# Four whole chunks beside nine pairs in the down stages of a two-layer encoder kernel

## The chip, the cores and the metric

The kernel is one program on one core of a Trainium2 chip. The metric is the device time of one execution in microseconds. The engines of the core work in parallel, each in the order of its own instruction queue: TensorE (PE: matmuls; PEld: its weight loads), VectorE (DVE), ScalarE (ACT), GpSimd (POOL) and SyncE (SP, which here issues DMAs). They wait for each other through semaphores. POOL issues DMAs too, among them those that add what they bring to what lies in SBUF (accumulating DMAs).

## The reference

An encoder of two layers on 512 positions of width 1024, all in float32. Each layer has two feed-forward parts, an attention part between them and an embedding gate at the end. The change touches the feed-forward parts alone, and of them the end of the up projection and the whole down projection:

```python
def swiglu(x, w_gate, w_up, w_down):
    return (jax.nn.silu(x @ w_gate) * (x @ w_up)) @ w_down

h = h + 0.5 * swiglu(rmsnorm(h, norm_ffn1[i]), ffn1_w_gate[i], ffn1_w_up[i], ffn1_w_down[i])
...
h = h + 0.5 * swiglu(rmsnorm(h, norm_ffn2[i]), ffn2_w_gate[i], ffn2_w_up[i], ffn2_w_down[i])
```

The inner width is 2816, so 22 chunks of 128. There are four such parts in the program, two in each layer.

## The kernel before

Every float32 operand of a matmul is split in two: a high half (`split`, L149, ScalarE) and what is left of it (L150, VectorE). A product is then three matmuls: high by high, high by low, low by high. Activations lie transposed, 128 features of a chunk on the partitions and the 512 positions along a row; the first 256 of a row are called `l`, the last 256 `r`.

`ffn` makes the 22 inner chunks `a[m]`, one after the other. For the first `FRONT` = 5 it calls `pair_front`, plain three-term products of 128x512. For the others it calls `pair_fast`, which needs fewer multiplications: it works on halves of the normalised input that `halves(c)` prepares for c = 0 to 3 after chunks 0 to 3 (`SUMS`), with matmuls of 128x256. For the pairs of chunks up to `READY`, `inner_sums` makes the combinations that the down stage needs; `SPLIT` = 2 chunks are split ahead of the last up chunk.

`down` multiplies by the down weights. It takes the chunks in pairs (A, B), `K2` = 11 of them, and the weights as four quarters b11, b12, b21, b22; each pair costs seven products where the plain way has eight. The pairs are worked off in units of two (six units, the last with one pair). A weight unit is 128x1024 (512 KB), loaded by SP into one of five buffers `wr` (`load`, L441) and split into `wh` and `wl`, four buffers each. Sums of quarters are not computed by an engine: after a unit has been split, an accumulating DMA of POOL adds the next quarter in place (`add`, L445), and the result is split again. The products (L454 to L456) go to two blocks of 128 positions each, in this order:

- phase 1: for each unit r1 with b11, r2 with b21, and one unit later r3 with b11+b12
- phase 2: rb with b12+b22 (two accumulates ahead: `summed`), one unit later r1 with that +b11, one more unit later rc with that +b21. The moving chunks of rb are `sums`, split as x3 when their unit comes.
- tail: r3 with b22.

In the tail the results are turned back by TensorE transposes (L537) to features by positions. `first_half` (chunks 0 to 3, after units 2 and 3): ScalarE takes the transposes out of PSUM with a factor 0.5 (L543), a POOL DMA adds the kept input h to it (L544), then `norm_split` starts the next part's norm (L212 on ScalarE, L213 on VectorE). `second_half` (chunks 4 to 7; the r columns after units 4 and 5, the l columns at the end): VectorE adds 0.5 times the transposes to h, which SP has loaded (L533, L554). At the end POOL stores all eight chunks (L572).

PSUM banks come from four pools (mm, sc, ob, tr in the profile's names); `tr` has two banks, which rb, the transposes and the norms share. The tile scheduler sets the order within each engine's queue.

## Time and profile before

| | us |
|---|---|
| median of 3 runs | 2117.63 |
| lowest and highest | 2116.38, 2119.2 |
| the profiled run | 2114.56 |
| its span in the trace | 2112.8 |

The four down stages lie at about 242 to 392, 897 to 1049, 1317 to 1466 and 1905 to 2059 us of the span. "Busy" is the time in which an engine executes; the granted clock is the share of TensorE's full clock that it had (1.00 is all of it). In a timeline, a bracket behind a row gives the idle time of that engine just before it and what released it. Names such as `wh` or `act` are the program's tiles; a DMA's row is at its issue, not at its landing.

### The profile page before, as it was taken

Reading aid. Unit: us, or ns where it says so; the run is one execution under the profiler, and the core shown is the slowest. Engines: PE = TensorE matmul, PEld = TensorE weight load, DVE = VectorE, ACT = ScalarE, POOL = GpSimd, SP = SyncE. Lnnn points to the kernel's source line nnn. Section 1 sums busy time; section 2 is a strip of 40 time slices with the busy share of each in tenths; the row PEclk is TensorE's granted clock in tenths of the full one; section 3 lists DMA queues with packets and bytes.
Section 4 is the critical chain, followed back from the end, with each engine's and each line's share of the span. In section 5 each row is a group of like instructions: output and inputs, shape, how many; then the busy total and the mean of one; then the engine's idle time right before and its main releaser. Section 6 shows DMA issues by size and latency. Waiting matters only on the chain.

```text
span 2112.8 us, 32943 instructions
## 1 busy us (share of the span) xinstructions
PE 2014.7 (95%) x12294; PEld 1786.2 (85%) x12294; DVE 1593.2 (75%) x2763; ACT 1134.0 (54%) x1918; POOL 305.5 (14%) x350
## 2 busy tenths in 40 slices
PE   8999989999999999989899999898999999999878
PEld 6999967778888899977688999687888889997666
DVE  8888965698766888876568888666787588888555
ACT  5455654487645455555454556555666445556542
POOL 0000021332212000011220000113000200002122
PEclk9999999999999999999999999999999999999999
DMA  6666698643425466589644765896333446658962
GB/s 194 171 181 182 171 190 214 178 97 75 102 64 169 124 179 179 162 204 201 190 163 127 183 185 160 204 213 189 107 110 96 160 115 185 181 154 194 184 200 80
DMA packets 128048, 339.09 MB, mean 160 GB/s; under 512 B 23824, under 2 KB 31504, under 8 KB 127888
## 3 DMA queue, kind: packets, MB, share of 16 engines
q1 hardware_dynamic: 95424, 237.32, 33.9%
q0 software_dynamic: 32320, 99.63, 27.2%
q8 instruction: 96, 1.57, 0.3%
q14 instruction: 64, 0.52, 0.1%
q10 hardware_dynamic: 144, 0.04, 0.0%
HBM read 308.62 MB, written 17.27 MB: 154 GB/s over the span
## 4 chain that ended last, share of the span: by engine, by line
PE 79%; DMA 8%; issue 5%; ACT 3%; DVE 3%; POOL 1%; SPq 0%; POOLq 0%; DVEq 0%; ACTq 0%
PE mm L365 6%; PE mm L363 6%; PE mm L364 6%; PE mm L175 6%; PE mm L174 6%; PE mm L176 6%; DMA wr<-in_dn_dram 5%; PE sc L364 3%; PE sc L365 3%; PE sc L363 3%; PE sc L176 2%; PE sc L174 2%; PE sc L175 2%; PE mm L454 2%; PE mm L455 2%
## 5 line engine op out<-in xcount | busy, mean ns | idle before, releaser
L149 ACT ACTIVATE wh<-wr 128x1024 fp32r<-128x1024 f32 (+1 forms) x503 | 515.4, 1029 | 511.1 <-DMA wr<-in_dn_dram 106.6
L150 DVE TENSOR_TENSOR wl<-wr,wh 128x1024 fp32r<-128x1024 f32 (+1 forms) x503 | 597.0, 1191 | 201.7 <-ACT wh L149 199.2
L365 PE MATMUL mm<-act,wl 128*128 128x256 f32 x1088 | 308.0, 283 | 0.0
L364 PE MATMUL mm<-act,wh 128*128 128x256 f32 x1088 | 308.0, 283 | 0.0
L363 PE MATMUL mm<-act,wh 128*128 128x256 f32 x1088 | 308.0, 283 | 0.0
L174 PE MATMUL mm<-act,wh 128*128 128x512 f32 (+1 forms) x648 | 256.5, 398 | 8.7 <-ACT act L212 7.6
L176 PE MATMUL mm<-act,wl 128*128 128x512 f32 (+1 forms) x648 | 256.8, 396 | 2.8 <-DVE wl L150 2.8
L175 PE MATMUL mm<-act,wh 128*128 128x512 f32 (+1 forms) x648 | 256.9, 397 | 1.3 <-DVE act L213 1.2
L363 PEld LDWEIGHTS mm<-act,wh 128*128 128x128 f32 x1088 | 208.9, 192 | 0.2
L364 PEld LDWEIGHTS mm<-act,wh 128*128 128x128 f32 x1088 | 208.9, 192 | 0.2
L365 PEld LDWEIGHTS mm<-act,wl 128*128 128x128 f32 x1088 | 208.9, 192 | 0.0
L341 POOL DMA_DIRECT2D wr<-in_gu_dram x68 | 59.3, 872 | 677.0 <-DVE wl L150 267.9
L365 PE MATMUL sc<-act,wl 128*128 128x256 f32 x544 | 154.0, 283 | 0.0
L364 PE MATMUL sc<-act,wh 128*128 128x256 f32 x544 | 154.0, 283 | 0.0
L363 PE MATMUL sc<-act,wh 128*128 128x256 f32 x544 | 154.0, 283 | 0.0
L174 PEld LDWEIGHTS mm<-act,wh 128*128 128x128 f32 x648 | 123.6, 191 | 33.9 <-ACT act L212 10.2
L175 PEld LDWEIGHTS mm<-act,wh 128*128 128x128 f32 x648 | 123.7, 191 | 26.3 <-DVE act L213 3.6
L176 PEld LDWEIGHTS mm<-act,wl 128*128 128x128 f32 x648 | 123.8, 191 | 26.1 <-DVE wl L150 3.9
L445 POOL DMA_DIRECT2D wr<-in_dn_dram x96 | 83.6, 925 | 420.9 <-DVE wl L150 342.1
L150 DVE TENSOR_TENSOR act<-act,act 128x512 fp32r<-128x512 f32 (+1 forms) x192 | 114.8, 622 | 3.6 <-ACT act L149 3.5
L149 ACT ACTIVATE act<-act 128x512 fp32r<-128x512 f32 (+1 forms) x192 | 103.0, 568 | 4.1 <-DVE act L1244 2.1
L365 PEld LDWEIGHTS sc<-act,wl 128*128 128x128 f32 x544 | 104.5, 192 | 0.0
(240 smaller groups left out, 4674.8 us busy)
## 6 DMA issues: line engine op xcount, KB each, us to landing
wr<-in_gu_dram SPq DMA_DIRECT2D x176, 512.0 KB, 4.3
wr<-in_dn_dram SPq DMA_DIRECT2D x80, 512.0 KB, 4.7
wr<-in_dn_dram POOLq DMA_DIRECT2D x80, 512.0 KB, 7.2
wr<-in_gu_dram POOLq DMA_DIRECT2D x68, 512.0 KB, 5.5
rb<-in_gu_dram SPq DMA_DIRECT2D x68, 256.0 KB, 2.5
act<-kept SPq DMA_DIRECT2D x44, 256.0 KB, 4.6
wr<-in_qk_ab_dram SPq DMA_DIRECT2D x20, 512.0 KB, 3.8
kept<-act POOLq DMA_DIRECT2D x32, 256.0 KB, 2.9
```

The lines of the kernel that those rows point to most:

```text
L149: self.put(self.nc.scalar.activation(hi, src, AF.Copy))
L150: self.put((lo_eng or self.nc.vector).tensor_tensor(lo, src, hi.bitcast(F32), op=ALU.subtract))
L174: mm(out, stat[0], mov[0], start=start, stop=False)
L175: mm(out, stat[0], mov[1], start=False, stop=False)
L176: return mm(out, stat[1], mov[0], start=False, stop=stop)
L341: nc.gpsimd.dma_start(rs, w[:, :UNIT], accum_op=ALU.add)
L363: mm(out, w[0][:, c], xs[k][0][:, x], start=start and k == 0, stop=False, skip_group_check=True)
L364: mm(out, w[0][:, c], xs[k][1][:, x], start=False, stop=False, skip_group_check=True)
L365: mm(out, w[1][:, c], xs[k][0][:, x], start=False, stop=stop and k == half - 1, skip_group_check=True)
L445: nc.gpsimd.dma_start(raw, b[:, u.start * T:u.stop * T], accum_op=ALU.add)
L454: mm(p, xh, wh, start=start and k == 0, stop=False, skip_group_check=True)
L455: mm(p, xh, wl, start=False, stop=False, skip_group_check=True)
```

## The change

The 22 chunks are no longer all paired. Chunks 0 to 3 (`WHOLE` = 4) are multiplied whole, each with two products of 128x512 for each half of the positions; the other 18 make `K2` = 9 pairs in five units (the last with one pair). The weights are laid out anew on the host: first the left and right halves for the whole chunks, then the four quarters of the pairs. The products of the whole chunks (24 matmuls each for the two units of one half of the weights) are placed so:

- right weights by the r positions, on a bank pair `rx`, at the very start, copied out to c5
- left weights by the l positions, on r2, between phase 1 and phase 2, behind the first `summed`
- left weights by the r positions, on rc, a unit after each of rb's first two units
- right weights by the l positions, on r3, ahead of b22.

r3 is no longer copied out after phase 1, but added to c5 by VectorE in phase 2; the subtraction of u3 from c5 is moved up.

In the up projection `FRONT` is 4, and chunk 4 is made by the new `pair`: three-term products whose first four input chunks come as the halves of `halves`, which for that keeps the r half (z) as well.

In the tail all eight kept chunks are loaded by SP ahead of b22's last unit. `second_half` on the r columns comes after b22's units 0 and 1, `first_half` after units 2 and 3, and VectorE adds the residual in both; L543 and L544 are gone.

```diff
-FRONT = 5
-READY = 9
-SPLIT = 2
+FRONT = 4
+WHOLE = 4
+READY = 6
+LEAD_X = 2
-K2 = NF // 2
+K2 = (NF - WHOLE) // 2
...
+    def pair(self, w, y, z):
+        nc, half = self.nc, KC // 2
+        pgu = []
+        for j in range(2):
+            u = self.unit(w[:, (1 - j) * UNIT:(2 - j) * UNIT])
+            p = self.sbank() if j else self.bank()
+            for k in (*range(half, KC - 1), *range(half), KC - 1):
+                c = (k + half * j) % KC * P
+                ww = u[0][:, c:c + P], u[1][:, c:c + P]
+                if k < half:
+                    for i, x in enumerate((y[k], z[k])):
+                        out = p[:, i * T // 2:(i + 1) * T // 2]
+                        mm = nc.tensor.matmul
+                        mm(out, ww[0], x[0], start=False, stop=False, skip_group_check=True)
+                        mm(out, ww[0], x[1], start=False, stop=False, skip_group_check=True)
+                        mm(out, ww[1], x[0], start=False, stop=False, skip_group_check=True)
+                else:
+                    self.mm3(p, ww, y[k], k == half, k == KC - 1)
+            pgu.append(p)
+        t = self.act()
+        nc.scalar.activation(t, pgu[0], AF.Silu)
+        nc.vector.tensor_tensor(t, pgu[1], t, op=ALU.mult)
+        return t
...
             if k < KC // 2:
-                both = self.act(F32R)
-                out.append((both[:, :H], both[:, H:]))
-                self.split(x[:, :H], *out[-1])
+                for xx in (x[:, :H], x[:, H:]):
+                    both = self.act(F32R)
+                    out.append((both[:, :H], both[:, H:]))
+                    self.split(xx, *out[-1])
...
+        rx = [self.tbank(), self.tbank()]
+        for u in wide:
+            for k in u:
+                xs[k] = xs[k] or self.split_chunk(a[k], nc.vector)
+            product(rx, u, self.parts(load(right, u)), xs, r, True, u.stop == WHOLE)
+        cx = copied(rx)
...
-        c1 = copied(r1)
-        for o, p in zip(c1, r2):
+        summed(0)
+        ws = [self.parts(load(left, u)) for u in wide]
+        for u, ww in zip(wide, ws):
+            product(r2, u, ww, xs, l, False, u.stop == WHOLE)
+        c11, c5 = copied(r1), cx
+        for o, p in zip(c11, r2):
             tt(o, p, o, op=ALU.add)
-        c11, c5 = c1, copied(r3)
...
-        summed(0)
         for s in range(n + 2):
             if s + 1 < n:
                 summed(s + 1)
...
+            if s < len(wide):
+                product(rc, wide[s], ws[s], xs, r, True)
+            if s == 1:
+                for o, p in zip(c5, r3):
+                    tt(o, p, o, op=ALU.add)
...
-        for m in range(M, KC):
+        for m in range(KC):
             nc.sync.dma_start(hs[m], kept[m])
...
-            nc.scalar.activation(h, p, AF.Copy, scale=0.5)
-            nc.gpsimd.dma_start(h, kept[m], accum_op=ALU.add)
+            nc.vector.scalar_tensor_tensor(h, p, 0.5, h, op0=ALU.mult, op1=ALU.add)
...
+        for u in wide:
+            product(r3, u, self.parts(load(right, u)), xs, l)
         for i, u in enumerate(units):
-            raw = load(b22, u)
-            product(r3, u, self.parts(raw), x4, l, False, True)
-            if i in (2, 3):
+            product(r3, u, self.parts(load(b22, u)), x4, l, False, last(u))
+            if i < 2:
+                second_half(M + 2 * i, c22, r)
+            elif i < 4:
                 first_half(2 * i - 4)
                 first_half(2 * i - 3)
-            elif i > 3:
-                second_half(M + 2 * i - 8, c22, r)
```

Three places show what this does to the queues, all in the first down stage. First ScalarE's queue where the up projection ends and the down stage begins. `wh` are the high halves of weight units, L387, L389 and L414, L416 the end of the last up chunk, the other `act` rows high halves of inner chunks. Before, in order:

```order
L149 ACTIVATE wh_2889<-wr_2879 128x1024
L149 ACTIVATE act_2881<-act_680 128x512
L389 ACTIVATE act_2700<-act_2700 128x512
L149 ACTIVATE wh_2905<-wr_2807 128x1024
L149 ACTIVATE act_2885<-act_932 128x512
L149 ACTIVATE wh_2931<-wr_2921 128x1024
L149 ACTIVATE act_2923<-act_1060 128x512
```

After, where L494 are the two copies of rx (banks tr_2828 and tr_2829) and act_2880 is the high half of A[0], the first that r1 needs:

```order
L416 ACTIVATE act_2721<-act_2721 128x512
L150 ACTIVATE wh_2941<-wr_2931 128x1024
L494 ACTIVATE act_2874<-tr_2828 128x512
L494 ACTIVATE act_2875<-tr_2829 128x512
L150 ACTIVATE act_2880<-act_678 128x512
L150 ACTIVATE wh_2968<-wr_2958 128x1024
L150 ACTIVATE act_2884<-act_833 128x512
```

The split of A[0], ahead of the down stage before, now stands behind copies that read the finished rx.

Second, ScalarE's queue at the passage from phase 1 to phase 2. L461 are the copies of r1 and r3; wh_3225 and wh_3255 are the first two units of b12+b22, wh_3272 the first with b11 added; act_3215, act_3220, act_3245, act_3250 are high halves of the first four of `sums`. Before:

```order
L461 ACTIVATE act_3196<-mm_2802 128x512
L149 ACTIVATE wh_3225<-wr_3209 128x1024
L149 ACTIVATE wh_3255<-wr_3212 128x1024
L461 ACTIVATE act_3201<-sc_2803 128x512
L461 ACTIVATE act_3202<-sc_2804 128x512
L149 ACTIVATE act_3215<-act_369 128x512
L149 ACTIVATE act_3220<-act_559 128x512
L149 ACTIVATE wh_3272<-wr_3209 128x1024
L149 ACTIVATE act_3245<-act_780 128x512
L149 ACTIVATE wh_3302<-wr_3242 128x1024
L149 ACTIVATE act_3250<-act_1032 128x512
```

After, where the two units of the left weights and the high halves of the first two of `sums` (act_3261, act_3266) stand just ahead; wh_3271 and wh_3313 are the first two units of b12+b22, wh_3344 the first with b11 added, act_3303, act_3308, act_3364, act_3369, act_3433 and act_3438 the high halves of the next six of `sums`, and the 128x256 rows those of x4:

```order
L150 ACTIVATE wh_3271<-wr_3209 128x1024
L150 ACTIVATE act_3303<-act_1309 128x512
L150 ACTIVATE wh_3313<-wr_3258 128x1024
L150 ACTIVATE act_3308<-act_1561 128x512
L150 ACTIVATE act_3364<-act_1813 128x512
L150 ACTIVATE act_3369<-act_2065 128x512
L150 ACTIVATE act_3424<-act_705 128x256
L150 ACTIVATE act_3427<-act_957 128x256
L150 ACTIVATE act_3433<-act_3071 128x512
L150 ACTIVATE act_3438<-act_3079 128x512
L150 ACTIVATE act_3493<-act_1209 128x256
L150 ACTIVATE wh_3344<-wr_3209 128x1024
```

The splits of the third to eighth of `sums` stood behind wh_3272 and now stand ahead of its counterpart wh_3344.

Third, POOL's queue in the tail: L445 or L478 the last accumulates of weights, then the DMAs on the chunks h. Before:

```order
L445 DMA wr_3427<-in_dn_dram 128x512
L544 DMA act_3611<-in_xT_dram 128x512
L572 DMA kept_2800<-act_3611 128x512
L544 DMA act_3612<-in_xT_dram 128x512
L572 DMA kept_2800<-act_3612 128x512
L544 DMA act_3613<-in_xT_dram 128x512
L572 DMA kept_2800<-act_3613 128x512
L544 DMA act_3614<-in_xT_dram 128x512
```

After:

```order
L478 DMA wr_3430<-in_dn_dram 128x512
L620 DMA kept_2821<-act_3614 128x512
L620 DMA kept_2821<-act_3615 128x512
L620 DMA kept_2821<-act_3616 128x512
L620 DMA kept_2821<-act_3617 128x512
```

The DMAs that add the kept chunks (L544) are gone from it; only the stores are left.

More of the change, by code (lines that the diff above doesn't have):

```diff
@@ L424, in inner_sums, with down @@
         return s
-    def down(self, w, a, x1, sums, kept):
+    def down(self, w, a, xs, sums, kept):
         nc, H = self.nc, T // 2
@@ L433, in down @@
         copy, tt, sub = nc.scalar.activation, nc.vector.tensor_tensor, ALU.subtract
-        A, B = a[0::2], a[1::2]
-        b11, b12, b21, b22 = (w[n] for n in range(4))
-        units = [slice(u, min(u + 2, K2)) for u in range(0, K2, 2)]
-        ks = lambda u: range(u.start, u.stop)
+        A, B = a[WHOLE::2], a[WHOLE + 1::2]
+        left, right = (w[:, n * WHOLE * T:(n + 1) * WHOLE * T] for n in range(2))
+        b11, b12, b21, b22 = (w[:, 2 * WHOLE * T:][:, n * K2 * T:(n + 1) * K2 * T] for n in range(4))
+        units = [range(u, min(u + 2, K2)) for u in range(0, K2, 2)]
+        wide = [range(u, u + 2) for u in range(0, WHOLE, 2)]
         def load(b, u):
-            raw = self.wr.tile([P, UNIT], F32, tag="wr", name=self.nm("wr"))[:, :(u.stop - u.start) * T]
+            raw = self.wr.tile([P, UNIT], F32, tag="wr", name=self.nm("wr"))[:, :len(u) * T]
             nc.sync.dma_start(raw, b[:, u.start * T:u.stop * T])
@@ L445, in add, with product @@
             nc.gpsimd.dma_start(raw, b[:, u.start * T:u.stop * T], accum_op=ALU.add)
-        def product(out, u, ws, xs, cols, start, stop):
+        def product(out, u, ws, xs, cols, start=False, stop=False):
             mm = nc.tensor.matmul
-            for j, k in enumerate(ks(u)):
+            for j, k in enumerate(u):
                 wh, wl = (x[:, j * T:(j + 1) * T] for x in ws)
@@ L465, in down, with summed @@
         r2 = [self.bank(), self.obank()]
-        x2, x3, x4 = ([None] * K2 for _ in range(3))
+        x1, x2, x3, x4 = ([None] * K2 for _ in range(4))
         n, raws = len(units), {}
+        last = lambda u: u.stop == K2
+        rx = [self.tbank(), self.tbank()]
[4 more added lines that the diff above has]
+        cx = copied(rx)
+        def summed(s):
+            raws[s] = load(b12, units[s])
+            add(raws[s], b22, units[s])
         for s in range(n + 1):
@@ L516, in down @@
                     tt(u3[i], c2[i], rb[i], op=sub)
+                for i in range(2):
+                    tt(c5[i], c5[i], u3[i], op=sub)
             if s > 1:
                 u = units[s - 2]
-                product(rc, u, self.parts(raws[s - 2]), x2, r, True, True)
-                for k in ks(u):
+                product(rc, u, self.parts(raws[s - 2]), x2, r, False, last(u))
+                for k in u:
                     t = self.act(F32R)
@@ L1369, in _quarters @@
 def _quarters(w):
[L1371 removed]
+    c = w.reshape(NF, P, 2, T)
+    whole = c[:WHOLE].transpose(1, 2, 0, 3).reshape(P, -1)
+    pairs = c[WHOLE:].reshape(K2, 2, P, 2, T).transpose(2, 1, 3, 0, 4).reshape(P, -1)
+    return np.concatenate([whole, pairs], axis=1)
 def _rows(w):
```

50 lines of the change are left out of this document (24 added, 26 removed).

## Prediction

> **What bounds the kernel now.** I read the page first, then busy time by windows, then the timelines around the idle spots.
>
> ```profile
> span 2112.8 us, 32943 instructions
> PE 2014.7 (95%) x12294; PEld 1786.2 (85%) x12294; DVE 1593.2 (75%) x2763; ACT 1134.0 (54%) x1918; POOL 305.5 (14%) x350
> PE 79%; DMA 8%; issue 5%; ACT 3%; DVE 3%; POOL 1%; SPq 0%; POOLq 0%; DVEq 0%; ACTq 0%
> ```
>
> TensorE is busy for 95% of the span, and 79% of the chain that ended last is its own. So two things can shorten the run: fewer matmuls, or less of the idle 5% and of the slow clock that comes with it. The change adds matmuls; what counts is where the idle time lies. The windows below cut out the four down stages, three rows each: phase 1 up to the first matmul of phase 2, phase 2, and the tail with the return to the next stage. Columns: length, busy time of each engine (with instructions), granted clock, DMA share. The last row, a stretch of the up projection, is there for comparison.
>
> ```profile
> 241.90:289.90 48.00, 45.11 (x200) 37.02 (x199) 37.62 (x56) 28.57 (x42) 8.50 (x10) 1.00 0.85 203
> 289.90:351.80 61.90, 54.95 (x234) 44.76 (x235) 37.71 (x50) 30.09 (x45) 11.48 (x14) 0.94 0.92 205
> 351.80:392.00 40.20, 31.77 (x163) 26.68 (x162) 19.63 (x37) 17.91 (x30) 7.89 (x12) 0.92 0.66 202
> 896.80:945.40 48.60, 45.11 (x200) 37.03 (x198) 37.62 (x56) 28.57 (x42) 8.76 (x10) 1.00 0.84 204
> 945.40:1006.80 61.40, 55.09 (x234) 44.79 (x235) 37.81 (x50) 29.98 (x45) 11.30 (x13) 0.94 0.93 206
> 1006.80:1049.00 42.20, 31.89 (x139) 23.83 (x138) 21.79 (x38) 18.99 (x32) 10.79 (x14) 0.92 0.58 175
> 1316.80:1364.50 47.70, 45.10 (x201) 37.02 (x199) 37.62 (x56) 28.56 (x42) 8.09 (x10) 1.00 0.84 201
> 1364.50:1425.30 60.80, 55.15 (x234) 45.17 (x235) 37.89 (x50) 30.45 (x45) 12.12 (x14) 0.94 0.93 213
> 1425.30:1466.00 40.70, 33.14 (x172) 27.80 (x171) 21.90 (x38) 18.82 (x31) 11.07 (x16) 0.92 0.63 185
> 1904.90:1952.20 47.30, 45.11 (x201) 37.02 (x199) 37.63 (x56) 28.58 (x42) 8.57 (x11) 1.00 0.85 203
> 1952.20:2016.00 63.80, 55.73 (x233) 45.33 (x234) 37.96 (x50) 30.20 (x45) 11.26 (x14) 0.92 0.91 198
> 2016.00:2059.00 43.00, 32.33 (x139) 25.05 (x138) 21.70 (x38) 18.93 (x32) 10.70 (x14) 0.88 0.59 178
> sum 605.60, PE 530.47 PEld 431.52 DVE 386.88 ACT 309.66 POOL 120.54; mean PE 44.21 PEld 35.96 DVE 32.24 ACT 25.80 POOL 10.04
> ...
> 664.00:725.00 61.00, 61.00 (x276) 50.46 (x275) 47.89 (x79) 27.99 (x40) 8.00 (x7) 1.00 0.52 147
> ```
>
> TensorE is idle for 605.60 - 530.47 = 75.1 us of these 605.6, which is most of the 98.1 us (2112.8 - 2014.7) that it is idle at all; the up stretch has none and a full clock. By kind of window: phase 1 11.2, phase 2 27.0, tail 37.0. Busy time at a clock below 1.00 is lost too; busy time times (1 - clock) gives 14.4 us in phase 2 and 11.6 in the tail, 26.0 together. So **about 101 us hang on the down stages**: 52.6 on the passage from phase 1 to 2 (11.2 + 27.0 + 14.4), 48.6 on the tail. TensorE at the passage of the first stage, with the idle time before a row and its releaser in brackets:
>
> ```profile
> 289.90 0.50 PE L454 MATMUL tr<-wh,act 128*128 128x512 f32 x1 [2.89 <-ACT act L149]
> 290.24 0.39 PE L455 MATMUL tr<-wl,act 128*128 128x512 f32 x1
> ...
> 292.53 0.39 PE L456 MATMUL tr<-wh,act 128*128 128x512 f32 x1
> 298.98 0.80 PE L454 MATMUL tr<-wh,act 128*128 128x512 f32 x1 [6.06 <-ACT act L149]
> 299.57 0.63 PE L455 MATMUL tr<-wl,act 128*128 128x512 f32 x1
> 300.00 0.63 PE L454 MATMUL tr<-wh,act 128*128 128x512 f32 x1
> ```
>
> From 290.24 to 292.53 there are ten starts at **0.229 us** each: the price of a 128x512 matmul. After the 6.06 us stall they come 0.43 apart; after the 2.89 us stall they don't. Both waits are for a split by ScalarE, whose queue shows why:
>
> ```profile
> 287.30 1.06 ACT L149 ACTIVATE wh<-wr 128x1024 fp32r<-128x1024 f32 x1 [1.31 <-DVE wl L150]
> ...
> 289.22 1.15 ACT L149 ACTIVATE act<-act 128x512 fp32r<-128x512 f32 x2
> 297.35 1.06 ACT L149 ACTIVATE wh<-wr 128x1024 fp32r<-128x1024 f32 x1 [6.98 <-DMA wr<-in_dn_dram]
> 298.31 0.61 ACT L149 ACTIVATE act<-act 128x512 fp32r<-128x512 f32 x1
> ```
>
> The split of rb's second unit (298.31) stands in the queue behind the split of a chained sum, which waits 6.98 us for its accumulating DMA. The tail on ScalarE:
>
> ```profile
> 353.18 0.58 ACT L543 ACTIVATE act<-tr 128x512 f32<-128x512 f32 x1
> ...
> 361.17 0.72 ACT L212 ACTIVATE act<-act,gain 128x512 fp32r<-128x512 f32 x1 [4.28 <-DMA act<-in_xT_dram]
> ...
> 375.88 0.72 ACT L212 ACTIVATE act<-act,gain 128x512 fp32r<-128x512 f32 x1 [6.49 <-DMA act<-in_xT_dram]
> ```
>
> L543 leaves TensorE's transposes at 353.18, the DMA that adds the residual lands before 361.17, and only then does the next norm's split (L212) run; the splits of weights stand behind it in the same queue. That serial trip of some 7 us is what the tail is made of.
>
> **The change, part by part.** *Added matmuls.* A pair of chunks costs 42 matmuls of 128x512 (seven products, two output blocks, three terms), a whole chunk 24. Before 11 x 42 = 462, after 9 x 42 + 4 x 24 = 474: 12 x 0.229 x 4 stages = **+11.0 us**. The new `pair` at m = 4 has 24 matmuls of 128x512 and 48 of 128x256 in place of 48 of 128x512. The 128x256 spacing is 0.12:
>
> ```profile
> 171.74 0.28 PE L363 MATMUL mm<-act,wh 128*128 128x256 f32 x1
> 171.86 0.28 PE L364 MATMUL mm<-act,wh 128*128 128x256 f32 x1
> ```
>
> So 48 x 0.12 - 24 x 0.229 = 0.26, times 4 **+1.1**. The added splits of z (four of 128x256 a stage on ScalarE and on VectorE) lie beside front matmuls, where VectorE is busy 47.89 of 61.00. Chunk 3's halves are needed after 9 wide and 18 narrow matmuls, 4.2 us into the pair, and take some 3 us on VectorE; without that cover it would be 1 to 2 us a stage. I take nothing.
>
> *A new wait, at the start of a stage.* ScalarE's order after the change has the two copies of rx (L494) ahead of the split of A[0], which the first matmul of r1 needs, and the copies wait for the end of rx. The nearest rows:
>
> ```profile
> 283.98 1.07 ACT L461 ACTIVATE act<-mm 128x512 f32<-128x512 f32 x2
> L149 ACT ACTIVATE act<-act 128x512 fp32r<-128x512 f32 x148 | 88.7, 617 | 4.1 <-DVE act L1244 2.1 <-DVE act L1055 2.0
> ```
>
> The second copy can start when rx's last matmul ends (0.39 after its start), takes some 0.55, then the split 0.62; TensorE would have gone on 0.23 after that start. 0.39 + 0.55 + 0.62 - 0.23 = 1.33 us a stage, **+5.3**. Bounds: 0, and 2.0 a stage if VectorE's low half were waited for too; four matmuls that need only the high half stand before it. What queues behind the copies (b21's split, more splits of A and B) is needed a unit of 5.5 us later.
>
> *The passage.* The 24 matmuls of the left product on r2 (5.5 us) now run while the first sums are made, and two blocks of 12 on rc (2.75 each) follow rb's first and second unit: 11.0 us of work that needs no sum. On ScalarE the high halves of `sums` for rb's first eight pairs now stand ahead of the first split that waits for a second accumulate (wh_3344); before, those of the third pair on stood behind it (wh_3272). Whether 11.0 is enough is a question of the DMAs. In the stretch 284 to 305:
>
> ```profile
> DMA packets 1201, 4.37 MB, mean 208 GB/s; under 512 B 138, under 2 KB 138, under 8 KB 1199
> q0 software_dynamic: 921, 3.34, 84.7%
> q1 hardware_dynamic: 278, 1.01, 16.1%
> ```
>
> Accumulates (q0) took 0.847 x 21 us for 3.34 MB, 2.8 us for 512 KB; plain loads (q1) 1.75. Phase 2 needs one load and three accumulates a unit, 10.1 us, against 36 x 0.229 = 8.2 of matmuls: 1.9 short. Over 5.5 units that is 10.5 us, and the idle time of phases 1 and 2 is 38.2 / 4 = 9.5. So before, **the passage is paid to the DMA queue**. After, 4.5 units are 8.6 us short, with 11.0 of cover. Phase 1 keeps its eleven loads of 512 KB (nine and rx's two) and has one accumulate fewer. I leave 2.0 us a stage for sums that come late singly: 52.6 - 8.0 = **-44.6**. Bounds: nothing left (-52.6), or one stall as long as the 6.06 with its slow matmuls (rival one).
>
> *The tail.* All 16 residual DMAs and their issues go; eight plain loads of kept chunks stand on SyncE's queue ahead of b22's last load, each waiting for a matmul of phase 2 that frees its buffer, some 20 us before it is read. `second_half` on the r columns runs after b22's first two units, `first_half` after the next two, and VectorE adds. Its price:
>
> ```profile
> L554 DVE SCALAR_TENSOR_TENSOR act<-tr,act 128x256 f32<-128x256 f32 x32 | 12.1, 417 | 5.5 <-PE tr L537 5.3
> L213 DVE SCALAR_TENSOR_TENSOR act<-act,gain,act 128x512 fp32r<-128x512 f32 x48 | 36.6, 770 | 47.2 <-ACT act L212 47.1
> ```
>
> At most 2 x 0.417 = 0.83 for 128x512, with 0.77 for L213: 3.2 us for a step's two chunks. A middle unit of b22 has 12 matmuls and 16 transposes, over 4 us, so VectorE keeps up. The last unit is short (6 matmuls, 1.4 us): the subtractions of r3 then queue behind up to 3.2 us of VectorE work, with the first matmuls of the next stage as cover. I leave 2.5 us a stage: 48.6 - 10.0 = **-38.6**. Bounds: 0 to 6 a stage.
>
> The Trainium skill speaks against this move: "ScalarE: Activation LUTs", section "Step-by-step: what each stage is for", holds that ScalarE lies closer to PSUM and VectorE to SBUF, and the change moves a PSUM read to VectorE. The rows agree in sign, 0.58 on ScalarE (L543) against up to 0.83; by the rule on the path, 16 x 0.25 = 4 us come back, and by the windows (VectorE 19.63 of 40.20 in the tail) none.
>
> **Sum.** 2114.56 us for the profiled run (span 2112.8 and 1.8 around it): + 11.0 + 1.1 + 5.3 - 44.6 - 38.6 = 2048.8. The median of the runs, 2117.63, is 3.1 above that run; with the same offset **2052**.
>
> **The rivals.** *One: the passage's stall only moves*, to r1's first unit, which needs b12+b22+b11 right after two rc blocks' worth of cover. For it: the DMA share of 0.92 in phase 2, no room to catch up. Against: the balance above. A 6.06 us stall with seven matmuls at 0.43 in place of 0.229 (1.4) is 7.5 instead of 2.0 a stage: +22, 2074; a stall of 4 a stage gives +8, 2060. I take 5.5 a stage, **2066**. The Trainium skill ("TensorE: Matmul & The Clock Gate", Part 1) lets the clock drop only after an idle window of about 3.4 us; the trace agrees (2.89 no, 6.06 yes), and by it a stall kept under 3.4 a stage adds no slow matmuls, at most 2058.
>
> *Two: half of the tail stays*, the chain from transposes over VectorE to L212 taking the DMA's place: 24 instead of 10, **2066**. For: L213 waits 47.1 us for L212 in all. Against: no step of it is over 1 us.
>
> *Three: slower.* Each of phase 2's 15 chained steps finds its sum late, since five buffers now also hold left's weights and a load waits for a buffer. Parity is (2117.6 - 2052) / 60 = 1.1 us a step; at 1.5 us, + 90, **2142**. For: the DMA share. Against: the 46 us after 299 in phase 2 of the first stage, which run without such waits on the same five buffers (54.95 busy of 61.90, with the 6.06 in it).
>
> *Four: nothing won*, the sums' waits and the tail's coming back whole elsewhere: **2117**.
>
> **How the numbers follow.** Forecast 0.60 (its own range 2040 to 2060, from the bounds of the new wait, passage and tail), rival one 0.20, two 0.12, three 0.05, four 0.03. The range holds the first three and their sum (2052 + 14 + 14 = 2080): 2038 to 2080. A measurement of this kernel can tell about 0.2%, 4 us: faster 0.92, same 0.03, slower 0.05.
>
> **What would show it.** TensorE's idle time in the three windows of each stage: near 1.3 at the start of r1, released by ScalarE; under 2 us before rb's and r1's first units; no releaser DMA on a kept chunk, and under 3 us in the tail. Clock near 1.00 throughout. I am wrong if r1's first unit waits over 4 us for a split behind an accumulate, if VectorE's subtractions hold the tail, or if `pair` waits for chunk 3's low halves.

## The result, and the profile after

| | us |
|---|---|
| median before (4 runs) | 2118.41 |
| median after (4 runs) | 2067.37 (2065.12 to 2069.41) |
| ratio, with its 95% interval | 0.9759 (0.9742 to 0.9776) |
| span of the profiled run after | 2067.6 |

The change takes 51 us off, where 66 were forecast: inside the range, and short of the forecast by a quarter. Medians and ratios here and below are of fast runs; one run of e6_x3, 3276.15 us at a granted clock of 0.555, is left out. The page of the changed kernel begins:

```profile
span 2067.6 us, 33144 instructions
PE 2013.6 (97%) x12438; PEld 1786.7 (86%) x12438; DVE 1595.9 (77%) x2743; ACT 1121.0 (54%) x1898; POOL 282.9 (14%) x318
PE 79%; DMA 7%; DVE 6%; issue 4%; ACT 3%; POOL 1%; SPq 0%; POOLq 0%; ACTq 0%; DVEq 0%
```

TensorE's idle time fell from 98.1 to 54.0 us, and its busy time hardly at all, although fewer of its matmuls are slow: there is more for it to do. VectorE is now in the chain of work that ended last with 6%, where it had 3%. The windows of the four down stages, three rows each: up to rb's first matmul, up to the tail's first matmul on r3, and the tail up to the next norm's scale (columns as in the prediction):

```profile
238.40:291.30 52.90, 49.33 (x212) 38.95 (x211) 39.85 (x59) 31.84 (x47) 6.80 (x8) 1.00 0.71 178
291.30:336.00 44.70, 43.66 (x187) 34.53 (x187) 23.95 (x33) 19.29 (x30) 10.63 (x13) 1.00 0.91 185
336.00:383.20 47.20, 45.22 (x263) 39.19 (x262) 35.88 (x58) 23.73 (x35) 5.95 (x10) 1.00 0.79 277
880.60:931.80 51.20, 49.31 (x212) 38.98 (x211) 39.45 (x58) 30.61 (x45) 6.93 (x8) 1.00 0.73 178
931.80:975.80 44.00, 42.55 (x188) 34.86 (x187) 24.73 (x33) 20.71 (x32) 10.47 (x12) 1.00 0.94 194
975.80:1021.10 45.30, 40.11 (x184) 31.25 (x182) 36.47 (x55) 22.90 (x35) 11.57 (x11) 0.96 0.72 259
1289.30:1340.00 50.70, 49.10 (x213) 39.00 (x211) 39.46 (x58) 30.18 (x44) 6.96 (x8) 1.00 0.72 177
1340.00:1387.50 47.50, 44.06 (x188) 36.01 (x187) 27.55 (x38) 23.15 (x34) 10.45 (x12) 0.96 0.94 197
1387.50:1428.90 41.40, 38.15 (x196) 32.17 (x194) 34.65 (x50) 20.32 (x30) 14.60 (x17) 0.96 0.71 249
1871.50:1923.40 51.90, 49.37 (x212) 38.93 (x212) 39.38 (x58) 30.18 (x44) 6.93 (x8) 1.00 0.72 178
1923.40:1971.30 47.90, 44.03 (x187) 35.98 (x186) 25.75 (x35) 22.34 (x34) 10.47 (x12) 0.96 0.89 183
1971.30:2013.90 42.60, 38.58 (x184) 30.13 (x183) 35.35 (x53) 21.93 (x33) 11.56 (x11) 1.00 0.86 303
sum 567.30, PE 533.48 PEld 429.99 DVE 402.45 ACT 297.20 POOL 113.32; mean PE 44.46 PEld 35.83 DVE 33.54 ACT 24.77 POOL 9.44
```

In the stages 33.8 us are idle (567.30 - 533.48), where it was 75.1; the clock is at 0.96 to 1.00. But in every stage idle time now lies inside phase 1. Each first row has 1.6 to 3.6 us of it; the first rows of the prediction had 2.2 to 3.5, but all of it was one wait at their end, for rb's first matmul.

To compare kernels with different numbers of matmuls I use one measure throughout: from the trace, the time from each matmul's start to the next, less what it takes back to back (0.227 us for 128x512, 0.12 for 128x256, 0.109 for a transpose), summed over a part of the four stages. It counts waits and slow matmuls alike, from one trace of each kernel. Phase 1 runs to the last matmul of the first r3 sums, phase 2 to r3's return in the tail, the tail to the next norm's scale:

| time lost, us, four stages | phase 1 | phase 2 | tail | span |
|---|---|---|---|---|
| before | -0.2 | 45.3 | 62.5 | 2112.8 |
| after | 13.6 | 17.7 | 24.0 | 2067.6 |

Passage (the first two) -13.8, tail -38.5, added matmuls +12.1: -40.2 of the -45.2 between the two spans (the medians lie 51 apart). The rest lies outside the down stages, some 3.5 us of it ahead of the first one, which begins at 238.4 instead of 241.9. By the same measure 2.14 us of that is a wait for a low half of a weight unit that ended at 48.90 us (1.98 us idle) and is gone; the matmuls behind it, 0.43 apart for 3.4 us, cost some 1.6 more.

### The profile page after: what moved, and what is told of

It reads as the page before. It is cut to its first block, busy times and chain, and to the rows that moved or that the text cites. A ratio compares the mean times of both kernels' runs of the same rounds, so it can differ in the third digit from the quotient of the medians.

```text
span 2067.6 us, 33144 instructions
## 1 busy us (share of the span) xinstructions
PE 2013.6 (97%) x12438; PEld 1786.7 (86%) x12438; DVE 1595.9 (77%) x2743; ACT 1121.0 (54%) x1898; POOL 282.9 (14%) x318
## 4 chain that ended last, share of the span: by engine, by line
PE 79%; DMA 7%; DVE 6%; issue 4%; ACT 3%; POOL 1%; SPq 0%; POOLq 0%; ACTq 0%; DVEq 0%
PE mm L391 6%; PE mm L390 6%; PE mm L392 6%; DMA wr<-in_dn_dram 5%; PE mm L176 5%; PE mm L175 5%; PE mm L177 5%; PE sc L392 3%; PE sc L391 3%; PE sc L390 3%; PE sc L175 2%; PE sc L177 2%; PE sc L176 2%; DVE wl L151 2%; PE ob L392 2%
## 5 line engine op out<-in xcount | busy, mean ns | idle before, releaser
L150 ACT ACTIVATE wh<-wr 128x1024 fp32r<-128x1024 f32 (+2 forms) x499 | 511.5, 1029 | 499.8 <-DMA wr<-in_dn_dram 126.5
L151 DVE TENSOR_TENSOR wl<-wr,wh 128x1024 fp32r<-128x1024 f32 (+2 forms) x499 | 594.2, 1195 | 190.5 <-ACT wh L150 186.2
L175 PE MATMUL mm<-act,wh 128*128 128x512 f32 (+1 forms) x632 | 247.5, 393 | 1.1 <-ACT act L213 0.5
L177 PE MATMUL mm<-act,wl 128*128 128x512 f32 (+1 forms) x632 | 247.4, 391 | 0.5 <-DVE wl L151 0.5
L176 PE MATMUL mm<-act,wh 128*128 128x512 f32 (+1 forms) x632 | 247.1, 392 | 0.6 <-DVE act L214 0.6
L390 PEld LDWEIGHTS mm<-act,wh 128*128 128x128 f32 x1088 | 208.9, 192 | 0.2
L391 PEld LDWEIGHTS mm<-act,wh 128*128 128x128 f32 x1088 | 208.9, 192 | 0.2
L392 PEld LDWEIGHTS mm<-act,wl 128*128 128x128 f32 x1088 | 208.9, 192 | 0.0
L176 PEld LDWEIGHTS mm<-act,wh 128*128 128x128 f32 x632 | 118.9, 188 | 23.9 <-DVE act L214 2.4
L175 PEld LDWEIGHTS mm<-act,wh 128*128 128x128 f32 x632 | 118.8, 188 | 23.7 <-ACT act L213 1.7
L177 PEld LDWEIGHTS mm<-act,wl 128*128 128x128 f32 x632 | 118.8, 188 | 22.3 <-DVE wl L151 1.3
L478 POOL DMA_DIRECT2D wr<-in_dn_dram x80 | 69.6, 944 | 420.5 <-DVE wl L151 319.6
L487 PE MATMUL mm<-wh,act 128*128 128x512 f32 x248 | 98.2, 396 | 13.8 <-DVE act L538 9.0
L151 DVE TENSOR_TENSOR act<-act,act 128x512 fp32r<-128x512 f32 (+1 forms) x176 | 105.9, 630 | 6.9 <-ACT act L150 6.9
L390 PEld LDWEIGHTS sc<-act,wh 128*128 128x128 f32 x544 | 104.4, 192 | 0.0
```

What stands on the lines that cost most here:

```text
L150: self.put(self.nc.scalar.activation(hi, src, AF.Copy))
L151: self.put((lo_eng or self.nc.vector).tensor_tensor(lo, src, hi.bitcast(F32), op=ALU.subtract))
L175: mm(out, stat[0], mov[0], start=start, stop=False)
L176: mm(out, stat[0], mov[1], start=False, stop=False)
L177: return mm(out, stat[1], mov[0], start=False, stop=stop)
L390: mm(out, w[0][:, c], xs[k][0][:, x], start=start and k == 0, stop=False, skip_group_check=True)
```

## The experiments

Two theories stood against each other for the passage. One: what waits is set by the order in the in-order queues of ScalarE and VectorE. Two: the chained sums' transfers pace phase 2, and a wait that is taken away there comes back at the next sum. For the tail the question was how much of its gain is the residual on VectorE. The same measure for all runs, with medians and the ratio to the kernel before on the same chip (what lies outside the stages differs by a few us between the traces, so a small difference between two spans says little):

| run | phase 1 | phase 2 | tail | span | median | ratio (95%) |
|---|---|---|---|---|---|---|
| e3_tail | -0.2 | 44.4 | 14.0 | 2060.1 | 2067.88 | 0.9776 (0.9745 to 0.9807) |
| e3b_residual | 0.5 | 44.9 | 30.1 | 2081.2 | 2082.56 | 0.9839 (0.9815 to 0.9864) |
| e4_oldtail | 14.3 | 11.9 | 86.4 | 2122.3 | 2128.8 | 1.005 (1.0027 to 1.0073) |
| e6_x3 | 0.5 | 34.2 | 61.4 | 2099.4 | 2107.72 | 0.9962 (0.994 to 0.9984) |
| e13_tail_x3 | -0.2 | 34.4 | 16.3 | 2054.2 | 2057.57 | 0.9727 (0.9699 to 0.9754) |
| e5_late_rc | 12.8 | 45.4 | 17.1 | 2091.8 | 2089.62 | 0.9877 (0.9848 to 0.9906) |
| e1_bank | 14.4 | 7.9 | 28.4 | 2065.8 | 2068.38 | 0.9775 (0.9743 to 0.9807) |
| e2_copies | -0.1 | 24.6 | 16.2 | 2056.7 | 2056.2 | 0.9723 (0.9695 to 0.9751) |
| e12_both | -0.1 | 13.9 | 24.2 | 2050.9 | 2055.21 | 0.9717 (0.9686 to 0.9749) |
| e14_early_wl | -0.1 | 15.1 | 20.2 | 2046.1 | 2048.95 | 0.9682 (0.9657 to 0.9707) |
| e7_front | 14.1 | 17.1 | 21.7 | 2064.2 | 2063.82 | 0.9748 (0.9725 to 0.9772) |

### The tail alone

On the kernel before, eleven pairs and all:

```diff
-        for m in range(M, KC):
+        for m in range(KC):
             nc.sync.dma_start(hs[m], kept[m])
...
-            nc.scalar.activation(h, p, AF.Copy, scale=0.5)
-            nc.gpsimd.dma_start(h, kept[m], accum_op=ALU.add)
+            nc.vector.scalar_tensor_tensor(h, p, 0.5, h, op0=ALU.mult, op1=ALU.add)
...
-            if i in (2, 3):
+            if i < 2:
+                second_half(M + 2 * i, c22, r)
+            elif i < 4:
                 first_half(2 * i - 4)
                 first_half(2 * i - 3)
-            elif i > 3:
-                second_half(M + 2 * i - 8, c22, r)
```

> The kernel before, with the new tail alone: all eight kept chunks loaded, the residual added by VectorE, second_half on the r columns after units 0 and 1 of b22, first_half after units 2 and 3. Theory one: the tail's serial trip through ScalarE, POOL's DMA and ScalarE is what it cost, 36 to 40 us less, 2079 to 2083 against 2118.4. Rival: part of the tail's wait was the chained sums or weights late from phase 2, which stay, 15 to 25 less, 2093 to 2103.

2067.88 us: below what either theory gave, and no different from the whole change (2067.37; the profiled run, at 2061.84, is the fastest of its four). The tail loses 14.0 us instead of 62.5, while the passage stays as it was (44.2 against 45.1). The tail windows of this run:

```profile
342.00:384.00 42.00, 41.89 (x250) 36.84 (x249) 31.58 (x51) 20.45 (x31) 5.92 (x10) 1.00 0.79 285
982.00:1019.80 37.80, 34.75 (x171) 28.09 (x170) 32.68 (x50) 20.13 (x31) 11.54 (x11) 1.00 0.78 280
```

TensorE is busy for 41.89 of 42.00 us in the first stage's tail, at full clock. So the nine-and-four split, with all its matmuls, nets nothing on top of the tail: -12.9 in the passage, +10.0 in the tail, +12.1 of matmuls.

The first two hunks without the third, so that the halves stay at their old places:

> The kernel before with the residual on VectorE and eight loads alone; the halves stay at their old places (first_half after units 2 and 3 of b22, second_half on the r columns after units 4 and 5). The whole new tail gave 2067.9. If the trip through POOL's DMA is all: 2066 to 2074. If the order of the halves has a share, since second_half stands nearer to the end: 2078 to 2090.

2082.56: two thirds of the tail's gain (62.5 to 30.1 lost) is the residual on VectorE, one third (16 us, 30.1 to 14.0) the order of the halves. The first prospect, that POOL's trip is all, fell. The step takes the copy off ScalarE and the DMA off POOL together; the two weren't tried apart. The other way round, the changed kernel with the old first_half (ScalarE's copy and POOL's DMA, four loads) at its new place:

```diff
-        for m in range(KC):
+        for m in range(M, KC):
             nc.sync.dma_start(hs[m], kept[m])
...
-            nc.vector.scalar_tensor_tensor(h, p, 0.5, h, op0=ALU.mult, op1=ALU.add)
+            nc.scalar.activation(h, p, AF.Copy, scale=0.5)
+            nc.gpsimd.dma_start(h, kept[m], accum_op=ALU.add)
```

> The changed kernel, with first_half as before: ScalarE takes the transposes, a DMA of POOL adds the kept chunk, four chunks loaded; the order of the halves stays new. If the residual on VectorE is what the tail gained: 30 to 40 us more, 2097 to 2107. If the new order of the halves alone did it (second_half early, first_half two units before the end): 5 to 15 more, 2072 to 2082.

2128.8, slower than the kernel before and 22 us above the upper prospect. TensorE's waits in the first stage's tail:

```profile
357.92 0.52 PE L175 MATMUL ob<-act,wh 128*128 128x512 f32 x1 [2.93 <-ACT act L213]
365.04 0.77 PE L175 MATMUL ob<-act,wh 128*128 128x512 f32 x1 [2.01 <-ACT act L213]
372.47 0.50 PE L175 MATMUL ob<-act,wh 128*128 128x512 f32 x1 [1.89 <-ACT act L213]
379.18 0.79 PE L175 MATMUL ob<-act,wh 128*128 128x512 f32 x1 [3.62 <-ACT act L213]
```

Each of the four chunks is waited for in turn by the next stage's first product. The old order had one and a half more units of b22 behind first_half to hide POOL's DMAs; here half a unit is left. With POOL's DMA the tail at its new places loses more than at the old ones (86.4 against 62.5), so the rest of the change needs VectorE's addition.

### The passage: order or transfers

On the kernel before, the splits of the first six of `sums` ahead of the first split that waits for a second accumulate (`issue_after` orders an instruction behind another in its engine's queue):

```diff
+        for k in range(6):
+            x3[k] = self.split_chunk(sums[k], nc.vector)
+        early = self.hi
...
-                product(r1, u, self.parts(raws[s - 1]), x3, r, False, True)
+                with self.tc.issue_after(early.ins) if s == 1 else ExitStack():
+                    ws = self.parts(raws[s - 1])
+                product(r1, u, ws, x3, r, False, True)
```

> The kernel before, with the splits of the first six of sums put ahead of the first split on ScalarE that waits for a second accumulate, and nothing else. Theory one (order in ScalarE's queue): the second stall of each passage (6.22, 5.84, 5.81, 7.83 us) goes with its slow matmuls, 25 to 33 us less, 2085 to 2093. Theory two (the accumulates pace phase 2, which is some 9.5 us short of transfers in each stage): TensorE waits at r1's first unit instead, about as long, 2110 to 2118.

2107.72, just under theory two's range. TensorE at the passage of the fourth stage, then ScalarE:

```profile
1954.37 0.79 PE L455 MATMUL mm<-wh,act 128*128 128x512 f32 x1 [4.45 <-ACT wh L149]
```

```profile
1943.48 3.23 ACT L149 ACTIVATE act<-act 128x512 fp32r<-128x512 f32 x6
1953.26 2.00 ACT L149 ACTIVATE wh<-wr 128x1024 fp32r<-128x1024 f32 x2 [6.55 <-DMA wr<-in_dn_dram]
```

The six splits run early, rb's second unit no longer waits, and r1's first unit waits 4.45 us for a sum instead. Of 45.3 us lost, order alone gives back 11, so theory one has a quarter. The opposite test is the changed kernel with the left product on rc at the end of phase 2, which keeps the new order and takes 5.5 us of work a stage out of the passage (it loads and splits the left weights a second time, behind the last units of phase 2):

```diff
-            if s < len(wide):
-                product(rc, wide[s], ws[s], xs, r, True)
...
-                product(rc, u, self.parts(raws[s - 2]), x2, r, False, last(u))
+                product(rc, u, self.parts(raws[s - 2]), x2, r, True)
...
+        for u in wide:
+            product(rc, u, self.parts(load(left, u)), xs, r, False, u.stop == WHOLE)
         c21 = [self.act(), self.act()]
```

> The changed kernel, with the left product on rc (24 matmuls) at the end of phase 2 instead of behind rb's first two units; the two units of left weights are loaded and split a second time for it, 1 MB more a stage. Theory one (queue order alone): phase 2 waits little longer, and the bank's additions are no longer waited for so early, 2060 to 2068. Theory two (these 5.5 us a stage are cover for transfers that are late): they come back as waits at r1's first units, 4 to 5.5 us a stage, 2083 to 2090.

2089.62, at theory two's upper end. TensorE and ScalarE at the passage of the second stage:

```profile
946.28 0.79 PE L487 MATMUL mm<-wh,act 128*128 128x512 f32 x1 [6.22 <-ACT wh L150]
```

```profile
945.17 2.00 ACT L150 ACTIVATE wh<-wr 128x1024 fp32r<-128x1024 f32 x2 [8.19 <-DMA wr<-in_dn_dram]
```

Phase 2 loses 45.4 us, as much as before the change (45.3), and the wait shown is at r1's first unit. So most of the passage was paid to the transfers, and what the change put against it is work that needs no sum: 22 us of such matmuls on rc (4 x 24 x 0.229) saved 27.7 us of waits and slow matmuls in phase 2. Phase 1 and the tail lose 0.8 and 6.9 less in e5 than in the changed kernel, so over the three parts the saving is 20.0.

### What the change added

Three waits of the changed kernel were not there before. First the start of a stage, TensorE and ScalarE in the first one (L494 are rx's copies):

```profile
243.65 0.39 PE L489 MATMUL tr<-wh,act 128*128 128x512 f32 x1
245.24 0.50 PE L487 MATMUL mm<-wh,act 128*128 128x512 f32 x1 [1.21 <-ACT act L150]
```

```profile
243.39 1.28 ACT L494 ACTIVATE act<-tr 128x512 f32<-128x512 f32 x2 [0.63 <-PE tr L489]
244.56 0.62 ACT L150 ACTIVATE act<-act 128x512 fp32r<-128x512 f32 x1
```

245.24 - 243.65 - 0.227 is 1.36 us, as in the prediction's working (1.33). Second, rc's first block, here in the third stage: TensorE, VectorE (L538 adds r2 into c11 and so frees the banks that rc takes), ScalarE:

```profile
1342.49 0.39 PE L489 MATMUL tr<-wh,act 128*128 128x512 f32 x1
1346.31 0.50 PE L487 MATMUL mm<-wh,act 128*128 128x512 f32 x1 [3.44 <-DVE act L538]
```

```profile
1342.63 1.23 DVE L151 TENSOR_TENSOR wl<-wr,wh 128x1024 fp32r<-128x1024 f32 x1 [3.06 <-ACT wh L150]
1343.77 0.68 DVE L151 TENSOR_TENSOR act<-act,act 128x512 fp32r<-128x512 f32 x1
1344.37 0.69 DVE L555 TENSOR_TENSOR act<-sc,act 128x512 f32<-128x512 f32 x1
1344.97 0.68 DVE L151 TENSOR_TENSOR act<-act,act 128x512 fp32r<-128x512 f32 x1
1345.57 0.68 DVE L538 TENSOR_TENSOR act<-mm,act 128x512 f32<-128x512 f32 x1
1346.17 0.68 DVE L538 TENSOR_TENSOR act<-ob,act 128x512 f32<-128x512 f32 x1
```

```profile
1341.54 1.06 ACT L150 ACTIVATE wh<-wr 128x1024 fp32r<-128x1024 f32 x1 [4.26 <-DMA wr<-in_dn_dram]
```

VectorE was idle for 3.06 us although r2 was done (its last matmul starts at 1339.77), since L538 stands behind the low half of the second sum, which waits for its transfer, and behind three more rows, 1.8 us. The cover itself waits for the transfers that it should cover. Third, in the tail of the second stage, TensorE and VectorE:

```profile
980.70 0.50 PE L488 MATMUL sc<-wl,act 128*128 128x512 f32 x1 [1.82 <-DVE wl L151]
```

```profile
975.49 1.28 DVE L564 TENSOR_TENSOR act<-act,tr 128x512 f32<-128x512 f32 x2
976.69 1.29 DVE L566 TENSOR_TENSOR act<-act,act 128x512 f32<-128x512 f32 x2
977.89 0.42 DVE L151 TENSOR_TENSOR act<-act,act 128x256 fp32r<-128x256 f32 x1
978.23 0.69 DVE L576 TENSOR_TENSOR act<-mm,act 128x512 f32<-128x512 f32 x1
978.83 0.68 DVE L576 TENSOR_TENSOR act<-ob,act 128x512 f32<-128x512 f32 x1
979.43 4.62 DVE L151 TENSOR_TENSOR wl<-wr,wh 128x1024 fp32r<-128x1024 f32 x4
```

The low half of the second right unit stands behind six additions and subtractions. Each was moved in turn. For the second, x3 for the first three units is split at once, and the low half of the second sum goes behind L538:

```diff
         for o, p in zip(c11, r2):
-            tt(o, p, o, op=ALU.add)
+            added = tt(o, p, o, op=ALU.add)
+        for k in range(6):
+            x3[k] = self.split_chunk(sums[k], nc.vector)
+        early = self.hi
...
-                product(rb, u, self.parts(raws[s]), x3, l, True, last(u))
+                product(rb, u, self.parts(raws[s], (early, added) if s == 1 else None), x3, l, True, last(u))
```

where `parts` then issues its high half behind `early` and its low half behind `added`; so are the low halves of the first x4.

> The changed kernel, with VectorE's two additions of r2 into c11 (which free the banks that rc takes) ahead of the low half of the second unit of b12+b22, instead of behind it. In the changed kernel TensorE waits for these additions 0.42, 1.61, 3.60 and 4.03 us in the four stages, 9.7 together. Theory one (queue order): these waits go, 2058 to 2061 us against 2067.4. Theory two (the accumulating DMAs pace phase 2): TensorE only reaches the second unit of rb earlier and waits there or at r1's first unit for the sums, 2064 to 2068.

Phase 2 loses 9.8 us less, as theory one says (7.9 against 17.7), but the tail 4.4 and phase 1 0.8 more, and the median is that of the changed kernel. For the time, theory two has it, though the loss came back in the tail and not at the units that it named; for the place, theory one. For the first wait, the copies go behind the second unit of phase 1:

```diff
-        cx = copied(rx)
...
                 product(r3, u, self.parts(raws[s - 1]), x1, r, True, last(u))
+            if s == 1:
+                cx = copied(rx)
```

> The changed kernel, with ScalarE's two copies of rx issued after the second unit of phase 1 instead of right behind rx. Theory one: the wait of 1.37 us at the start of each stage goes and nothing takes its place, 5.5 us less, 2062. Theory two: phase 1 ends at the accumulate of its last unit, which some stages already wait for (1.99 and 0.97 us), so that this wait grows by what is won, 2065 to 2067.

2056.2: 11 us less, twice the wait itself. Phase 1 loses nothing at all (13.6 to -0.1): the waits at its end, for the accumulate of its last unit, came with the copies' place in the queue, and were not set by the transfers, as theory two had it. Its last two accumulates are issued 33.5 to 35.5 us into the changed kernel's stages, and 29.5 to 31.8 here; that is more than the 1.4 us of the wait, and why is open. Phase 2 loses 6.9 more, at rc's first block (4.06 us behind the same two additions in the first stage), and the tail 7.8 less. Both edits:

> The changed kernel with both edits: rx's copies late, and r2's additions ahead of the second unit's low half. With the copies alone late, TensorE still waits 4.22, 3.88, 4.49 and 3.77 us ahead of rc's first block, 16.4 together. Theory one (queue order on ScalarE and VectorE, not the transfers): these go, 2040 to 2044 us. Theory two (the transfers pace phase 2): the waits move on to the next units and the tail, 2050 to 2057.

2055.21, no measurable step beyond the copies alone: phase 2 gains 10.7 and the tail gives back 8.0, part of it because TensorE now reaches the tail before VectorE is through with its additions. So the third wait was moved as well:

```diff
-                for i in range(2):
-                    tt(c5[i], c5[i], u3[i], op=sub)
...
-        for i in range(2):
-            tt(c21[i], rc[i], u3[i], op=ALU.add)
...
             product(r3, u, self.parts(load(right, u)), xs, l)
+        with self.tc.issue_after(self.lo.ins):
+            for i in range(2):
+                tt(c5[i], c5[i], u3[i], op=sub)
+            for i in range(2):
+                tt(c21[i], rc[i], u3[i], op=ALU.add)
```

> The changed kernel with both edits of before (copies of rx late, r2's additions early) and a third: the subtractions of u3 from c5 and the additions that make c21 stand behind the low half of the second right unit in VectorE's queue, not ahead of it. With two edits TensorE waits 1.48, 2.20 and 2.21 us for that low half in three stages, 5.9 us. If that queue is the cause: 2048 to 2051. If VectorE is simply short of time there, the waits move behind the transposes: 2053 to 2057.

**2048.95**, in the range that names the queue: 18 us below the changed kernel and below both. The waits of 1.48, 2.20 and 2.21 us are gone from the trace; two of 1.23 and one of 0.78 us ahead of the transposes have come (times lost by the measure). By the measure the last step takes 4.0 off the tail and 2.8 off the stages in all; by the two ratios, whose intervals overlap, it alone isn't clear of noise. In phase 2 the main waits left are at r1's first unit, 0.70, 2.00 and 1.91 us in three stages, for the split of a chained sum: there the transfers do set the pace. Its page:

```profile
span 2046.1 us, 33135 instructions
PE 2004.3 (98%) x12438; PEld 1784.8 (87%) x12438; DVE 1591.9 (78%) x2743; ACT 1118.9 (55%) x1898; POOL 283.5 (14%) x318
```

### Without whole chunks, and without the new pair

> The kernel before with eleven pairs, with the new tail and the early splits of sums together, without whole chunks and without the new pair. The tail alone gave 2067.9, the early splits alone some 9 us. If the two add up: 2057 to 2061, below the changed kernel, which would say that the whole chunks cost more than they bring as they stand. If the passage is bound by transfers once the tail no longer hides anything: 2064 to 2069.

2057.57: the two add up. Eleven pairs with the new tail and early splits, three small edits on the kernel before, beat the change as made by 10 us in the medians (ratio 0.9727 against 0.9759, with overlapping intervals) and lose to it by 9 once its queues are in order (0.9682).

> The changed kernel with chunk 4 by pair_front as before, and one half of halves instead of two: the new pair alone is undone, and FRONT is 5. By the count of matmuls 1.1 us less. If the new pair also took away the wait of 2.14 us for a low half near 46 us of the first stage (which the kernel before has and the changed one has not): 1 us more. 2065 to 2069, and which of the two is told by the wait near 46 us in the profile.

2063.82, 3.5 us below the changed kernel, which its interval doesn't set clearly apart from it; and the wait that ended at 48.90 us has not come back. So the new pair is not what took it away. What did wasn't tried; in the changed kernel the first `inner_sums`, which are VectorE's, come after chunk 5 and not after chunk 1.

## Why the prediction was right, and where it was short

- *The whole.* The forecast for the profiled run's span was 2047.0 (2048.8 less 1.8), and 2067.6 came, 20.6 more: 17.0 from the passage, 8.5 from phase 1, 0.1 from the tail, and 5.0 less from outside the stages, which the sum did not have. The medians lie 15 apart.
- *Added matmuls* (+12.1): 144 more in all, as counted (12438 against 12294). Their price is a count times 0.229 and 0.12; no run shows it by itself (e7, 1.1 by the count, isn't clear of noise).
- *The tail* (-38.6 forecast, -38.5 measured). The mechanism, the serial trip over ScalarE and POOL's DMA, is shown by e3b and e4 for two thirds of it; the order of the halves, which the sum did not price by itself, is the rest. The close figure is luck, the sum of two errors: the tail alone is worth 48.5 on the kernel before, 10 more than I dared, and with the split it loses 10 of that again, which I hadn't in the sum. Part of these 10 is what the split puts on VectorE at the tail's start (waits of 1.98, 1.82 and 0.64 us for the low half; 4.0 us came off when six of the instructions ahead of it were moved); the rest wasn't traced to one cause. VectorE's addition takes 0.685 us for 128x512 against ScalarE's 0.578. The Trainium skill ("ScalarE: Activation LUTs", section "Step-by-step: what each stage is for") holds that ScalarE lies closer to PSUM, and these rows agree in sign. At 16 x 0.107 us that is 1.7 us at most, against the 32 that the step won.
- *The new wait at the start* (+5.3). Its own size was right, 1.36 to 1.37 in all four stages. Costing it alone was wrong: I took what queues behind the copies to be needed late enough, but the last accumulates of phase 1 are issued some 4 us later into the stage than with the copies out of the way, and phase 1 lost 13.6, all of which goes with the copies.
- *The passage* (-44.6): **the step that failed.** 27.6 were won in phase 2. Of the 17 missing, 7.3 were never there: I multiplied busy time by the share of clock missing in a window, 14.4, but the clock is low during the stalls too; by the spacing, 45.3 was lost in phase 2, not 52.6. The other 9.7 are the difference between 8.0 left and 17.7 found. My balance of transfers against cover was right (e5: take the cover away and the loss is back), but I took the two rc blocks as free to run, and their banks hang on two additions in VectorE's queue: e1, which moves them, loses 9.8 less in phase 2. I had named what queues behind waiting instructions on ScalarE, and not on VectorE; the bank's owner was no part of my list.
- *The rivals.* One, at 2066, has about the time and half the story: a wait did come back in the passage, at rc's first block behind a sum's split, not at r1's first unit. Two has about the time as well: the tail still loses 24.0 us, of 62.5 by the spacing, where the forecast left 10 of 48.6. But the end of its chain is not what TensorE waits for: no wait of over 0.3 us is for the norm's split on ScalarE. The longest are for the low half above, for the sums of squares of the next norm (2.87 us) and its scale (1.76 us twice). Three and four didn't occur: phase 2's later sums come in time, and 51 us were won.
- *The signs.* The wait at the start of r1 (1.20 to 1.21 us idle, released by ScalarE) and rb's and r1's first units (no wait of over 0.35 us) are as announced. The tail idles for 2.0, 5.2, 3.3 and 4.0 us in the rows above, where under 3 was named, and VectorE's subtractions do stand in its way, those of u3 ahead of the right weights' low half and not those of r3. That the matmuls behind a stall of under 3.4 us are never slow, as the prediction has it from two stalls, does not hold in its own trace; the last section has the rows.

With the three queues put in order the kernel is at 2049, 18 us lower, so queue order cost more than the 15 us missing. That this is near the forecast of 2052 is in part chance: phase 2 wins 30.2 and not 44.6, and the tail (42.3 against 38.6), phase 1 (nothing lost, where 5.3 was in the sum) and what lies outside the stages (6.4 less, which was not in it) make up for it.

## What to carry to other kernels

Before a block of work is placed to cover a wait, list everything that it needs itself, the PSUM bank it takes over and the engine that frees it included, and see whether any of it queues behind the wait that it should cover. A change of several parts is worth splitting even when it wins: here one part (the tail) made the whole gain, and the other (the whole chunks) came out even until three groups of instructions were moved. A short wait at the start of a chain of transfers can cost more than its length: here 1.4 us in each of four stages came with 13.6 us lost.

## What was not expected of the hardware

After the 3.44 us stall of the third stage TensorE's first matmuls start 0.23 to 0.34 us apart, and only then some eight come 0.43 apart (1347.4 to 1350.8), about 1.6 us lost: the slow clock sets in a microsecond after the stall has ended, and the rows right behind it don't show it.

The length of the stall does not decide it either. In the trace before, the 1.98 us of idle time that end at 48.90 are followed by matmuls 0.43 apart, and the 3.50 us that end at 945.41 are not. TensorE alone, in stretches of 3.41 us set by where the granted clock changes, first before around 48.90, then before around 945.41, then after around 1346.31 (length, busy time, granted clock, DMA):

```profile
45.95:49.36 3.41, 1.43 (x7) 1.00 0.00 0
49.36:52.77 3.41, 3.41 (x10) 0.50 0.75 222
940.24:943.66 3.42, 1.67 (x8) 1.00 1.07 255
943.66:947.07 3.41, 1.66 (x7) 1.00 1.03 268
947.07:950.48 3.41, 1.35 (x6) 1.00 1.04 202
950.48:953.89 3.41, 0.00 (x0) 0.50 1.06 209
1343.89:1347.30 3.41, 0.99 (x4) 1.00 1.01 156
1347.30:1350.72 3.42, 3.42 (x9) 0.50 1.00 188
```

The clock falls, for a whole stretch, behind stretches with 1.98, 2.06 and 2.42 us idle (the second holds the start of the next stall). The 3.50 us stall is cut in two by the border at 943.66, 1.75 us on either side, and no slow stretch follows the first of these two, nor the second. The Trainium skill ("TensorE: Matmul & The Clock Gate", Part 1) speaks of a free-running window of about 3.4 us, and the trace agrees with its length. But the window ahead of a fall is not wholly idle here: 1.43 us of one were busy. How much idle time it takes, and whether it is the same everywhere, these few stalls do not show.
